# A channel mixer in rounds of two pairs of blocks, its first operands made during the output projection

## The chip, the cores and the metric

The kernel runs on one core of one Trainium2 chip. The core has a matrix engine TensorE (PE, with its weight loads listed as PEld), three engines for elementwise work, VectorE (DVE), ScalarE (ACT) and GpSimd (POOL), and SyncE (SP), whose queue issues the kernel's transfers in program order. The metric is the time of one launch on the device in microseconds (us).

## The reference

One layer of an encoder over 2048 tokens of width 1024, in float32: two kinds of attention side by side, one output projection over both, and a channel mixer with hidden width 4096.

```python
mixed = jnp.concatenate([out_a, out_b], axis=-1)      # attention A and B, 2048 x 1024
x = x + jnp.einsum('bse,ed->bsd', mixed, w_out[l])
h = rmsnorm(x, mlp_norm_g[l])
u = jnp.einsum('bsd,df->bsf', h, w_up[l])
u = jnp.square(jax.nn.relu(u))
x = x + jnp.einsum('bsf,fd->bsd', u, w_down[l])
```

`rmsnorm(x, g)` is x / sqrt(mean(x²) + 1e-6) · g over the width. The result must agree with float32, so each operand of a product is split into a high part `hi` (ACT cast) and the rest `lo` (DVE subtraction), and a product is three matmuls: hi·hi, hi·lo, lo·hi.

## The kernel before

Projections and attention come first and take the time up to about 1820 us. The diff touches what follows.

**Output projection** (`out_proj`). 8 chunks of 256 tokens, two blocks of 128 each. For a chunk, 8 slices `m_raw` are loaded from DRAM, scaled by factors that PE spreads over the partitions (`pr`, lines 662 and 667) and split into `m_hi`, `m_lo`. For a block, 48 matmuls (`py`, line 680) of 128x512 give two halves of the row, DVE adds them to `xo` (line 684), the sum goes to DRAM (`x_d`), is squared and summed by ACT (line 156), multiplied in place by scale and gain (line 161), transposed by PE in eight pieces (`pt`, line 166), copied to `h_f` (lines 691 and 693) and stored to `hb_d`. A scheduler sets the order of instructions on each engine here; a pool with one or two buffers makes a tile wait until its readers are done.

**Channel mixer.** Both products use a Winograd form of Strassen's scheme: a 2x2 block product takes 7 products instead of 8, with operands that are sums of blocks. The 2x2 blocks of the transposed h are B11 to B22, their sums T1 to T4; the sums are formed by POOL from blocks that are loaded again (`h_raw`, `mlp_sums`), stored as `ht_d`, and loaded as operands `hop_T`, `hop_B` of 1 MB, which are split in place.

`mlp_up` (written in its own order, with no scheduler). 32 units: 2 halves of 1024 tokens by 16 slices of w_up. Each unit has 7 products of 12 matmuls (`psX`, `psY`, `psZ`, line 789). w_up of a unit comes as one transfer `wu_raw` of 1 MB, its sums `w_sum` are made by POOL (lines 718 to 721), 7 operands are split into `wu_hi`, `wu_lo` one unit ahead. DVE and ACT evict, square, and POOL sums of the results go to `us_d`. At the first unit four operands are loaded (`hop_T` three times, `hop_B`); in the last unit of the first half all seven are loaded anew.

`mlp_down` (its own order too). 7 right operands of 16 pieces, 8 blocks of tokens for each: 56 steps of 48 matmuls (`pd`, line 1001). In a step `u_raw` of 1 MB for the step after next is loaded, that of the next is split, and pieces of the next right operand are made: one in each of steps 1 to 6 and ten in the last. A piece of a T operand is a difference of two weight blocks, taken by POOL (line 951; T2 has two, lines 947 and 948, and goes to `wt_d`, from where T4 reads it).

## Time and profile before

| | |
|---|---|
| time, median of 3 runs | 3384.73 us (3384.37 to 3384.82) |
| the profiled execution | 3386.51 us, span 3384.70 us |
| PE busy | 3227.7 us, 95% |
| DVE, ACT, POOL busy | 60%, 45%, 48% |
| mean granted PE clock | 0.97 |

A busy share says how much of a time an engine has instructions under way. The granted clock is the share of full speed that PE was given: 1.00 is 2.4 GHz. In the timeline, a bracket behind an instruction names the time for which the engine had stood, and what it waited for. The name left of an arrow in a row is the tile written, those to its right are read; SPq is SyncE's queue.

### The profile page before, as it was taken

How to read it: one execution, taken by the hardware profiler on the slowest of the kernel's cores; microseconds unless marked ns; L12 is line 12 of the kernel's file. 1: busy time of each engine (PE TensorE's matmuls, PEld its weight loads, DVE VectorE, ACT ScalarE, POOL GpSimd, SP SyncE). 2: the span in 40 equal slices, each digit the busy share in tenths (PEclk: the TensorE clock that was granted, in tenths of full speed). 3: DMA queues.
4: the chain of work that ended last, by engine and by line, in shares of the span. 5: the costliest groups of instructions: out<-in, count | busy, mean ns of one | idle time of the engine just before them, and what ended most of it. 6: DMA issues, size and time to landing. Idle time of an engine off the chain costs nothing. (4 is left out here: it accounts for less than half of the span.)

```text
span 3384.7 us, 43164 instructions
## 1 busy us (share of the span) xinstructions
PE 3227.7 (95%) x15584; PEld 2459.7 (73%) x15584; DVE 2042.2 (60%) x3800; ACT 1530.4 (45%) x2344; POOL 1631.6 (48%) x894
## 2 busy tenths in 40 slices
PE   7999989999999999999999985999799999999999
PEld 6888866666666666666667774888688878788887
DVE  6545547777877777777866554554555544546542
ACT  4222226666666666666664222444444443222221
POOL 3344425666676666666665114556466521234200
PEclk9999989999999999999998997999899999899999
DMA  6336290122112210211113677455555465855653
GB/s 202 105 103 210 87 248 15 30 60 81 29 38 76 68 29 29 68 41 29 30 50 122 216 221 230 137 153 156 190 152 156 140 211 186 287 209 203 216 190 103
DMA packets 407894, 431.91 MB, mean 128 GB/s; under 512 B 26080, under 2 KB 343648, under 8 KB 395776
## 3 DMA queue, kind: packets, MB, share of 16 engines
q1 hardware_dynamic: 407680, 429.16, 40.7%
q8 instruction: 122, 2.00, 0.2%
q14 instruction: 92, 0.75, 0.1%
HBM read 287.45 MB, written 150.01 MB: 129 GB/s over the span
## 5 line engine op out<-in xcount | busy, mean ns | idle before, releaser
L545 POOL TENSOR_TENSOR acc<-acc,pta 128x1024 f32<-128x1024 f32 x224 | 535.1, 2389 | 258.6 <-ACT pta L543 253.7
L421 DVE CUSTOM_DVE_ANT_0 Sm<-ps_s,T 128x512 f32<-128x512 f32 x512 | 338.2, 685 | 124.9 <-PE ps_s L416 122.8
L543 ACT ACTIVATE pta<-ps_a 128x512 f32<-128x512 f32 x512 | 292.3, 594 | 208.9 <-PE ps_a L542 195.9
L509 DVE TENSOR_REDUCE mxa<-ps_m 128x1 f32<-128x512 f32 x512 | 330.5, 682 | 59.2 <-PE ps_m L506 57.6
L441 POOL TENSOR_TENSOR Sm<-Sm 128x2048 f32<-128x2048 f32 x64 | 294.4, 4600 | 139.0 <-ACT Sm L440 139.0
L1001 PE MATMUL pd<-wd_lo,u_hi 128*128 128x512 f32 x896 | 353.7, 395 | 6.0 <-DVE wd_lo L150 5.8
L1001 PE MATMUL pd<-wd_hi,u_hi 128*128 128x512 f32 x896 | 352.2, 393 | 7.2 <-ACT wd_hi L149 6.9
L1001 PE MATMUL pd<-wd_hi,u_lo 128*128 128x512 f32 x896 | 351.4, 392 | 2.5 <-DVE u_lo L150 2.5
L416 PE MATMUL ps_s<-Kb,Qb 128*128 128x512 f32 x1024 | 307.1, 410 | 2.4 <-DVE mx L421 2.3
L432 ACT ACTIVATE Sm<-Sm,negm 128x2048 f32<-128x2048 f32 x128 | 256.6, 2005 | 88.1 <-DVE negm L430 80.4
L552 PE MATMUL po_a<-pta,v_a 128*64 128x512 f32 x1024 | 279.7, 620 | 1.9 <-ACT pta L543 1.8
L541 PEld LDWEIGHTS ps_a<-Qa,Ka 128*128 128x128 f32 x512 | 96.2, 188 | 228.4 <-issue 196.3
L149 ACT CAST u_hi<-u_raw 128x1024 fp32r<-128x1024 f32 x112 | 112.2, 1050 | 311.9 <-PE pd L1001 277.8
L541 PE MATMUL ps_a<-Qa,Ka 128*128 128x512 f32 x512 | 233.6, 457 | 17.7 <-DVE vt L150 13.6
L789 PE MATMUL psY<-hop_T,wu_hi 128*128 128x512 f32 x768 | 237.6, 391 | 5.3 <-DVE u L799 5.3
L150 DVE TENSOR_TENSOR tl<-ptb,th 128x512 fp32r<-128x512 f32 x256 | 175.2, 684 | 79.7 <-ACT th L149 79.6
L470 PE MATMUL po_b<-th,Vb 128*128 128x256 f32 x1024 | 209.9, 288 | 9.3 <-ACT th L149 9.0
L416 PEld LDWEIGHTS ps_s<-Kb,Qb 128*128 128x128 f32 x1024 | 179.8, 191 | 47.4 <-DVE mx L421 11.0
L506 PE MATMUL ps_m<-Ka,Qa 128*128 128x512 f32 x512 | 202.5, 435 | 5.8 <-DVE mx L421 1.2
L470 PEld LDWEIGHTS po_b<-th,Vb 128*128 128x128 f32 x1024 | 173.1, 191 | 44.0 <-ACT th L149 14.7
L1001 PEld LDWEIGHTS pd<-wd_lo,u_hi 128*128 128x128 f32 x896 | 169.5, 189 | 48.9 <-DVE wd_lo L150 14.2
L1001 PEld LDWEIGHTS pd<-wd_hi,u_hi 128*128 128x128 f32 x896 | 169.4, 189 | 46.4 <-ACT wd_hi L149 11.3
(231 smaller groups left out, 7445.0 us busy)
## 6 DMA issues: line engine op xcount, KB each, us to landing
u_raw<-us_d SPq DMA_DIRECT2D x56, 1024.0 KB, 5.8
wd_raw<-in_w_down SPq DMA_DIRECT2D x176, 256.0 KB, 5.6
wu_raw<-in_w_up SPq DMA_DIRECT2D x32, 1024.0 KB, 5.9
us_d<-us SPq DMA_DIRECT2D x128, 256.0 KB, 3.4
us_d<-c SPq DMA_DIRECT2D x96, 256.0 KB, 3.8
Qb<-qkT_d SPq DMA_DIRECT2D x128, 128.0 KB, 3.0
Qa<-qkT_d SPq DMA_DIRECT2D x48, 256.0 KB, 4.8
m_raw<-mix_d SPq DMA_DIRECT2D x96, 128.0 KB, 3.6
```

The costliest lines, as they stand in the source:

```text
L416: nc.tensor.matmul(ps, Q[:, c, i, qb * P : (qb + 1) * P], K[c][:, ks], start=(i == 0), stop=(i == 1))
L421: nc.vector.tensor_tensor_reduce(out=Sm[:, ks], in0=ps, in1=T[t0][:, o - t0 : o - t0 + 512], scale=1.0, scalar=BIGNEG, op0=ALU.add, op1=AL ...
L432: nc.scalar.activation(Sm, Sm, AF.Exp, bias=negm, accum_out=l)
L441: nc.gpsimd.tensor_tensor(Pm[0], Pm[0], Pm[1], ALU.add)
L470: nc.tensor.matmul(po, V[a][:, kb, :], b[:, kk, :], start=(kb == 0 and n == 0), stop=(kb == NT - 1 and n == 2),)
L509: nc.vector.tensor_reduce(mx[:, kk : kk + 1], ps, AX.X, ALU.max)
L541: nc.tensor.matmul(ps, K[:, ks], Q[:, i, :], start=True, stop=False)
L543: ex = nc.scalar.activation(pt[:, i, :], ps, AF.Exp)
L545: nc.gpsimd.tensor_tensor(acc, prev if kb == 1 else acc, pt, ALU.add)
L552: nc.tensor.matmul(po[i * HD : (i + 1) * HD, :], v_a[:, kb, g * HD : (g + 1) * HD], pt[:, i, :], start=(kb == 0), stop=(kb == NT - 1),)
L789: nc.tensor.matmul(ps, w[:, j, :], b[:, h, j, :], skip_group_check=not start, start=(start and j == 0 and k == 0), stop=(j == 3 and k == 2),)
L1001: nc.tensor.matmul(ps, a[:, k, :], w, start=(k == 0 and q == 0), stop=(k == NK - 1 and q == 2))
```

## The change

Output projection: a chunk's operands are made one chunk before its blocks (`prepare`), the norm scale goes by ACT from `xt` into `h_f`, the gain is a column multiplied in behind the transposes, `h_f` has one buffer instead of two; sums are formed from `h_f` and two blocks loaded earlier (`h_old`) instead of four loaded again. The first two tiles of w_up and three operands are loaded and split in this stage; three products (36 matmuls) stand before the last block's transposes.

Up projection: pairs of units run in rounds of 14 items, the first three products of both and then the last four of both (`ROUND`). Operands of the left are split 8 items ahead, results are stored 2 to 5 items late. The four late operands of the first half are loaded at the start of `mlp_up` and split at items 2, 4, 5 and 6; those of the second half are loaded one by one behind the product that used them last, and split 5 items later. The last round loads and splits the first operands of the down projection.

Down projection: another order of the right operands; T2's weights are computed in the first 16 steps; additions with U and the second subtraction of T2 are POOL's; loads of pieces are spread over steps, and pairs use two buffers `wd_b`. Pools are taken from both ends of SBUF. The numbers of matmuls stay: 768, 2688 and 2688.

```diff
-            m2b, xp, hp, gp = pool("om_b", 1), pool("ox", 2), pool("oh", 2), pool("og", 1)
-            stage, m2a, mp, sm = pool("ows", 1), pool("om_a", 1), pool("om", 7), pool("osm", 2)
...
+            m2b, xp, hp, hsp, stage = pool("om_b", 1), pool("ox", 2), pool("oh", 1), pool("ohs", 3), pool("ows", 1)
...
+                chunks[tc_] = mh, ml
...
+            def block(tc_, b, before=None):
...
+                if before:
+                    before()
+                self.dma(self.x1_d[rows, :], xt)
+                hf = hp.tile([P, ND, P], F32, name="h2_f")
+                flat = hf.rearrange("p j t -> p (j t)")
+                ss = small.tile([P, 1], F32, name="h2_ss")
+                nc.scalar.activation(flat, xt, AF.Square, accum_out=ss)
+                r = self.rstd(small, ss, 1, 1.0 / D, "h2")
+                nc.scalar.activation(flat, xt, AF.Copy, scale=r)
+                def put(half, pt):
+                    sl = slice(half * 4, half * 4 + 4)
+                    g = gain[:, sl].rearrange("p (j o) -> p j o", o=1).broadcast_to([P, 4, P])
+                    nc.vector.tensor_tensor(hf[:, sl, :], pt, g, ALU.mult)
+                self.transposes(flat, pst, put)
+                c, th, s_ = r0 // 1024, (r0 // 512) % 2, (r0 // P) % 4
+                ts = slice(s_ * P, s_ * P + P)
+                for dh in range(2):
+                    self.dma(self.hb_d[c, 2 * dh + th, :, :, ts], hf[:, dh * 4 : dh * 4 + 4, :])
+                if th:
+                    old = stage.tile([P, 2, 4, P], F32, name="h_old", tag="stage")
                     for dh in range(2):
+                        self.dma(old[:, dh], self.hb_d[c, 2 * dh, :, :, ts])
+                    new = lambda: hsp.tile([P, 4, P], F32, name="h_sum")
+                    done = lambda i, t: self.dma(self.ht_d[c, i, :, :, ts], t)
+                    self.right_sums(old[:, 0], hf[:, 0:4], old[:, 1], hf[:, 4:8], new, done)
...
+            prepare(0)
+            for tc_ in range(8):
+                if tc_ < 7:
+                    prepare(tc_ + 1)
+                else:
+                    self.mlp_begin(early)
                 if tc_ == 4:
+                    self.up_load(0)
+                    self.up_load(1)
+                    self.B[0] = {n: self.operand(0, n) for n in self.RIGHT[:3]}
+                if tc_ == 5:
+                    self.up_sums(0, 0)
+                    self.up_sums(0, 1)
+                    self.up_sums(1, 0)
+                block(tc_, 0)
+                block(tc_, 1, self.mlp_first if tc_ == 7 else None)
...
+    LEFT = ("A11", "A12", "S2", "S3", "S1", "S4", "A22")
+    RIGHT = ("B11", "B21", "T2", "T3", "T1", "B22", "T4")
...
+        if n in self.RIGHT[:3]:
+            t = self.first.tile([P, 2, 4, 512], F32R, name=f"hop_{n}", tag="big")
+        else:
+            t = self.big.tile([P, 2, 4, 512], F32R, name=f"hop_{n}", tag="big")
...
+    ROUND = [(e, i) for lo, hi in ((0, 3), (3, 7)) for e in range(2) for i in range(lo, hi)]
+    def item(self, s):
+        d, r = divmod(s, 14)
+        e, i = self.ROUND[r]
+        return 2 * d + e, i
...
+    def up_split(self, s):
+        if s < 14 * self.NF:
+            n, i = self.item(s)
+            t = self.small_slot().rearrange("p h (j f) -> p h j f", f=P)
+            self.split(t[:, 0], t[:, 1], self.ops[n][self.LEFT[i]])
+            self.W[s] = t
...
+    def mlp_begin(self, early):
+        early.close()
+        self.wop = [self.right("uw", 7)]
+        self.acc = [self.right("psua", 3, space=PSUM)]
+        for s in range(7):
+            self.up_split(s)
+    EARLY = (0, 1, 3)
+    def mlp_first(self):
+        for s in self.EARLY:
+            self.up_product(s)
...
+        for s in self.EARLY:
+            after(s)
+        for n in self.RIGHT[3:]:
+            self.B[0][n] = self.operand(0, n, both=False)
+        splits = {2: "T3", 4: "T1", 5: "B22", 6: "T4"}
+        for s in range(7, 9):
+            self.up_split(s)
+        d = 14
+        done = 14 * (self.NF - 1)
+        for s in range(last + 1):
+            n, i = self.item(s)
+            r, n0 = s % d, 2 * (s // d)
+            if s not in self.EARLY:
+                self.up_product(s)
+                if s == last:
+                    self.down_early(r)
+                after(s)
+            if s > 0:
+                self.up_split(s + 8)
+            if s in splits:
+                self.in_place(self.B[0][splits[s]])
+            if r == 0:
+                self.up_sums(n0 + 1, 1)
+            elif r == 1:
+                self.up_load(n0 + 2)
+            elif r == 5:
+                self.up_load(n0 + 3)
+                self.up_sums(n0 + 2, 0)
+                self.up_sums(n0 + 2, 1)
+            elif r == 8:
+                self.up_sums(n0 + 3, 0)
+            if n == self.NF - 1:
+                name = self.RIGHT[i]
+                t = self.operand(1, name, both=False)
+                self.B.setdefault(1, {})[name] = t
+                later(s + 5, lambda t=t: self.in_place(t))
+            if done <= s < last:
+                self.down_early(r)
+            for f in todo.pop(s, ()):
+                f()
+        for k in range(10, 16):
+            self.fill_piece(0, k)
+        for s in sorted(todo):
+            for f in todo[s]:
+                f()
+    ORDER = ("B11", "B21", "B22", "T2", "T3", "T1", "T4")
...
+    TERMS = {"B11": ("11",), "B21": ("21",), "B22": ("22",), "T2": ("00",), "T3": ("22", "12"), "T1": ("12", "11"), "T4": ("21", "00")}
...
+    def prepare_piece(self, i, k):
+        terms = self.TERMS[self.ORDER[i]]
+        a = self.da.tile([P, 512], F32, name="wd_a")
+        self.dma(a, self.w_down(terms[0], k)[:, 0])
+        if len(terms) > 1:
+            b = self.db.tile([P, 512], F32, name="wd_b")
+            self.dma(b, self.w_down(terms[1], k)[:, 0])
+            self.nc.gpsimd.tensor_tensor(a, a, b, ALU.subtract)
+        self.pending[i, k] = a
+    def prepare_early(self, k):
+        t = self.raws.tile([P, 4, 512], F32, name="wd_raw", tag="raw")
+        self.dma(t, self.w_down(self.TERMS[self.ORDER[0]][0], k, 4))
+        for q in range(4):
+            self.pending[0, k + q] = t[:, q, :]
...
+    def u_load(self, m):
+        if m < len(self.STEPS):
+            i, b = self.STEPS[m]
+            t = self.first.tile([P, 2, 4, 512], F32R, name="u_op", tag="big")
+            self.U[m] = t.rearrange("p h a (k t) -> p h (a k) t", t=P)
+            self.dma(self.U[m][:, 1], self.us_d[self.RIGHT.index(self.ORDER[i]), b])
+    def u_split(self, m):
+        if m < len(self.STEPS):
+            self.in_place(self.U[m])
+    def down_early(self, r):
+        if r in (3, 4, 5):
+            self.u_load(r - 3)
+        if r in (2, 6, 10):
+            self.prepare_early({2: 0, 6: 4, 10: 8}[r])
+        if r in (6, 8):
+            self.u_split(r // 2 - 3)
+        for k in {7: (0, 1), 8: (2,), 9: (3,), 10: (4,), 11: (5,), 12: (6,), 13: (7, 8, 9)}.get(r, ()):
+            self.fill_piece(0, k)
+        if r == 13:
+            self.prepare_early(12)
...
+                if n != "B22":
+                    plus(t, t, U[b], nc.gpsimd)
...
+            def t2(k):
+                a, b, c = self.da.tile([P, H], F32, name="wd_a"), *(self.db.tile([P, H], F32, name="wd_b") for _ in range(2))
+                self.dma(a, self.w_down("12", k)[:, 0])
+                self.dma(b, self.w_down("11", k)[:, 0])
+                self.dma(c, self.w_down("22", k)[:, 0])
+                nc.gpsimd.tensor_tensor(a, a, b, ALU.subtract)
+                nc.gpsimd.tensor_tensor(a, c, a, ALU.subtract)
+                return lambda: self.dma(self.wt_d[k], a)
+            behind = []
+            for m, (i, b) in enumerate(self.STEPS):
+                if m:
+                    self.u_load(m + 2)
+                if m < 16:
+                    behind.append(t2(m))
+                if i < 6:
+                    for k in (6, 7) if b == 6 else (b,) if b < 6 else ():
+                        self.prepare_piece(i + 1, k)
+                    for k in {5: (8, 9, 10), 6: (11, 12), 7: (13, 14, 15)}.get(b, ()):
+                        self.prepare_piece(i + 1, k)
+                if m:
+                    self.u_split(m + 1)
+                if i < 6:
+                    for k in range(6, 16) if b == 7 else (b - 1,) if b else ():
+                        self.fill_piece(i + 1, k)
```

PE at the end of the output projection, before: `py` is the projection's result, `pt` the transposes of the last two blocks, `psX` the first product of the up projection.

```order
L680 MATMUL py<-wo_hi_17869,m_hi 128x512
L680 MATMUL py<-wo_lo_17870,m_hi 128x512
L680 MATMUL py<-wo_hi_17869,m_lo 128x512
L166 MATMUL pt<-ident,xo 128x128 x16
L789 MATMUL psX<-hop_B_19342,wu_hi 128x512 x2
L789 MATMUL psX<-hop_B_19342,wu_lo 128x512
```

PE at the same place, now (`w_op` is a split operand of w_up, `hop_B` and `hop_T` the operands of h):

```order
L691 MATMUL py<-wo_hi_17872,m_lo 128x512
L846 MATMUL psY<-hop_B_19261,w_op 128x512 x12
L846 MATMUL psX<-hop_B_19265,w_op 128x512
L171 MATMUL pt<-ident,h_f 128x128 x8
L846 MATMUL psX<-hop_B_19265,w_op 128x512 x11
L846 MATMUL psY<-hop_B_19261,w_op 128x512 x12
L171 MATMUL pt<-ident,h_f 128x128 x8
L846 MATMUL psY<-hop_T_19269,w_op 128x512 x12
L846 MATMUL psX<-hop_B_19265,w_op 128x512 x12
L846 MATMUL psY<-hop_T_19269,w_op 128x512 x12
L846 MATMUL psY<-hop_T_20218,w_op 128x512 x12
L846 MATMUL psZ<-hop_T_20220,w_op 128x512 x12
```

Three products now stand ahead of the last transposes and between them; the transposes of the last block come after 36 matmuls, and `hop_T_20218`, the first late operand (T3), is the fourth item behind them.

SP in the output projection, before, about two blocks whose sums are formed:

```order
L55 DMA xo<-in_x 128x1024
L55 DMA ht_d<-h_sum 512x1x128
L55 DMA hb_d<-h_f 512x1x128 x2
L55 DMA ht_d<-h_sum 512x1x128
L55 DMA x_d<-xo 128x1024
L55 DMA ht_d<-h_sum 512x1x128
L55 DMA h_raw<-hb_d 128x4x128
L55 DMA ht_d<-h_sum 512x1x128
L55 DMA h_raw<-hb_d 128x4x128
```

SP there, now:

```order
L58 DMA hb_d<-h_f 512x1x128
L58 DMA m_raw<-mix_d 128x256
L58 DMA hb_d<-h_f 512x1x128
L58 DMA ht_d<-h_sum 512x1x128
L58 DMA x_d<-xo 128x1024
L58 DMA m_raw<-mix_d 128x256
L58 DMA ht_d<-h_sum 512x1x128 x2
L58 DMA m_raw<-mix_d 128x256
L58 DMA ht_d<-h_sum 512x1x128
L58 DMA hop_T_19269<-ht_d 128x2048
```

The four `h_raw` loads behind a store are gone; `hb_d` of a block still stands among the stores of sums of the block before it.

SP from the last blocks to the up projection's operands, before:

```order
L55 DMA hb_d<-h_f 512x1x128
L55 DMA h_raw<-hb_d 128x4x128
L55 DMA ht_d<-h_sum 512x1x128 x2
L55 DMA h_raw<-hb_d 128x4x128
L55 DMA ht_d<-h_sum 512x1x128
L55 DMA wu_raw<-in_w_up 128x8x256
L55 DMA ht_d<-h_sum 512x1x128 x4
L55 DMA wu_raw<-in_w_up 128x8x256
L55 DMA hop_T_20174<-ht_d 128x2048
L55 DMA hop_T_20182<-ht_d 128x2048
L55 DMA hop_T_20190<-ht_d 128x2048
L55 DMA hop_B_20198<-hb_d 128x2048
```

SP there, now:

```order
L58 DMA hb_d<-h_f 512x1x128 x2
L58 DMA ht_d<-h_sum 512x1x128 x4
L58 DMA h_old<-hb_d 128x4x128 x2
L58 DMA hb_d<-h_f 512x1x128 x2
L58 DMA ht_d<-h_sum 512x1x128 x4
L58 DMA hop_T_20218<-ht_d 128x2048
L58 DMA hop_T_20220<-ht_d 128x2048
L58 DMA hop_B_20222<-hb_d 128x2048
L58 DMA hop_T_20224<-ht_d 128x2048
L58 DMA wu_raw<-in_w_up 128x8x256
```

The transfers of w_up are no longer between the last sums and the operands; the late operands still come behind the last four stores of sums.

## Rows read from the trace of the kernel before

**Rows 1.** Page, part 1: busy us and share of the span, of each engine
```profile
PE 3227.7 (95%) x15584; PEld 2459.7 (73%) x15584; DVE 2042.2 (60%) x3800; ACT 1530.4 (45%) x2344; POOL 1631.6 (48%) x894
```

**Rows 2.** Stretches: from:to, length, busy us (records) by engine, PE clock, DMA share, GB/s
```profile
2735.00:2780.00 45.00, 38.52 (x147) 27.68 (x146) 26.71 (x29) 22.37 (x34) 6.26 (x4) 0.92 0.80 279
...
2915.00:2970.00 55.00, 48.69 (x180) 35.30 (x179) 32.80 (x36) 15.13 (x20) 18.46 (x13) 0.84 0.86 304
2970.00:3190.00 220.00, 220.00 (x972) 182.19 (x971) 115.58 (x108) 59.57 (x76) 70.24 (x43) 1.00 0.58 203
3190.00:3230.00 40.00, 37.09 (x161) 29.53 (x160) 25.69 (x27) 13.83 (x19) 11.90 (x8) 1.00 0.67 239
...
2400.00:2470.00 70.00, 52.28 (x197) 41.12 (x196) 41.23 (x35) 33.17 (x44) 34.94 (x21) 0.85 0.61 207
2470.00:2735.00 265.00, 265.00 (x1171) 219.43 (x1170) 132.44 (x163) 125.11 (x220) 157.02 (x107) 1.00 0.50 147
2060.00:2130.00 70.00, 31.90 (x124) 25.29 (x125) 31.35 (x31) 24.38 (x34) 32.85 (x22) 0.71 0.62 200
```

**Rows 3.** Chain of waits, up projection: start, us, engine, result, line, instructions
```profile
2455.32 2.72 PE psX L789 x12
```

**Rows 4.** Timeline of PE: start, us, instruction, in brackets the idle time before
```profile
2059.20 0.40 PE L680 MATMUL py<-wo_hi,m_lo 128*128 128x512 f32 x1
2061.08 1.09 PE L166 MATMUL pt<-ident,xo 128*128 128x128 f32 x8 [1.48 <-DVE xo L161]
```

**Rows 5.** Waits of PE, 1980 to 2460: us in total, times, longest
```profile
PE psX L789 <- ACT wu_hi L149: 17.0, 1, 17.0
PE psX L789 <- ACT p L837: 16.6, 2, 10.5
PE pt L166 <- DVE xo L161: 9.4, 2, 8.0
```

**Rows 6.** Timeline of DVE, 1850 to 1863: end of the first block
```profile
1850.53 0.69 DVE L684 TENSOR_TENSOR xo<-py,xo 128x512 f32<-128x512 f32 x1 [0.68 <-PE py L680]
```

**Rows 7.** Groups by line, output projection, 1850 to 2060: busy, mean ns, idle before
```profile
L680 PE MATMUL py<-wo_hi,m_hi 128*128 128x512 f32 x240 | 98.6, 411 | 7.8 <-ACT m_hi L149 6.1 <-DVE xo L684 1.5
...
L161 DVE SCALAR_TENSOR_TENSOR xo<-xo,h_r,g_mlp 128x1024 f32<-128x1024 f32 x15 | 19.9, 1324 | 51.9 <-DMA x_d<-xo 51.9
...
L156 ACT ACTIVATE h_f<-xo 128x1024 f32<-128x1024 f32 x15 | 15.9, 1062 | 38.5 <-DVE xo L684 31.9 <-DMA hb_d<-h_f 3.2 <-DMA xo<-in_x 2.3
```

**Rows 8.** DMA issues, 1850 to 2060: count, KB, median us to landing
```profile
hb_d<-h_f SPq DMA_DIRECT2D x28, 256.0 KB, 4.5
```

**Rows 9.** Timeline of all engines, 2088.4 to 2100: the late operands
```profile
2088.45 2.41 SPq L55 DMA_DIRECT2D hop_T<-ht_d  x3
...
2097.68 1.90 ACT L149 CAST hop_T<-hop_T 128x2048 fp32r<-128x2048 f32 x1 [3.51 <-DMA hop_T<-ht_d]
...
2099.61 2.29 DVE L150 TENSOR_TENSOR hop_T<-hop_T 128x2048 fp32r<-128x2048 f32 x1 [2.14 <-ACT hop_T L149]
```

**Rows 10.** DMA issues, 2395 to 2450: operands of the second half
```profile
hop_T<-ht_d SPq DMA_DIRECT2D x4, 1024.0 KB, 13.8
```

**Rows 11.** Page, part 6: DMA issues of the weights, down projection
```profile
wd_raw<-in_w_down SPq DMA_DIRECT2D x176, 256.0 KB, 5.6
```

**Rows 12.** Groups by line, down projection, 2750 to 3380
```profile
L951 POOL TENSOR_TENSOR wd_raw<-wd_raw 128x512 f32<-128x512 f32 x48 | 78.5, 1643 | 146.5 <-DMA wd_raw<-in_w_down 77.2 <-DMA wd_raw<-wt_d 66.6 <-DVE wd_lo L150 2.5
...
L891 DVE TENSOR_TENSOR x<-x,U 128x512 f32<-128x512 f32 x24 | 19.2, 798 | 0.8
```

**Rows 13.** Groups by line, up projection, 2470 to 2735: w_sum on POOL
```profile
L720 POOL TENSOR_TENSOR w_sum<-wu_raw 128x512 f32<-128x512 f32 x13 | 16.9, 1298 | 25.0 <-DVE wu_lo L150 25.0
```

**Rows 14.** Timeline of POOL, 2097 to 2112
```profile
2102.59 3.25 POOL L720 TENSOR_TENSOR w_sum<-wu_raw 128x512 f32<-128x512 f32 x1 [3.70 <-DVE wu_lo L150]
```

**Rows 15.** Timeline of all engines, 1957 to 1966: end of put, stores
```profile
1957.61 0.68 DVE L691 COPY h_f<-pt 128x512 f32<-128x512 f32 x1
...
1965.13 1.33 SPq L55 DMA_DIRECT2D hb_d<-h_f  x2
```

More of the change, by code (lines that the diff above doesn't have):

```diff
@@ L150, in split, with norm_transpose @@
         self.nc.vector.tensor_tensor(lo, src, as32(hi), ALU.subtract)
-    def norm_transpose(self, xt, out, pool, pst, name, put, gain=None):
+    def norm_transpose(self, xt, out, pool, pst, name, put):
         nc = self.nc
@@ L582, in row_sums, with out_proj @@
         nc.vector.reciprocal(l, l)
[L585 removed]
+    def out_proj(self):
         nc, tc, ap = self.nc, self.tc, self.ap
@@ new lines, in fill_piece @@
+    def fill_piece(self, i, k):
+        if not self.quad(i, k):
+            self.D[i, k] = self.small_slot()
+        elif k % 4 == 0:
+            t = self.big.tile([P, 2, 4, 512], F32R, name="wd_q", tag="big")
+            for q in range(4):
+                self.D[i, k + q] = t[:, :, q, :]
+        w = self.D[i, k]
+        self.split(w[:, 0], w[:, 1], self.pending.pop((i, k)))
+    STEPS = [(i, b) for i in range(7) for b in range(8)]
+    def u_load(self, m):
[4 more added lines that the diff above has]
+            self.dma(self.U[m][:, 1], self.us_d[self.RIGHT.index(self.ORDER[i]), b])
@@ L898, in x1 @@
                     return None
-                half, dh = goes[order[i]]
+                half, dh = goes[n]
                 t = xp.tile([P, H], F32, name="x1")
                 self.dma(t, self.x1_d[rows(half, b), dh * H : dh * H + H])
+                if n != "B22":
+                    plus(t, t, U[b], nc.gpsimd)
                 return t
             def finish(i, b, ps, t):
-                n = order[i]
+                n = self.ORDER[i]
+                store = lambda half, dh, t: (lambda: self.dma(out[0, rows(half, b), dh * H : dh * H + H], t))
@@ L917, in finish @@
[L917 to L919 removed]
+                    if n == "T2":
+                        plus(y12[b], y12[b], U[b], nc.gpsimd)
                 else:
                     plus(t, ps, t)
[L922 removed]
                     if n == "T1":
                         plus(y12[b], ps, y12[b])
[L925 to L928 removed]
@@ L1004, in build @@
+                for f in behind:
+                    f()
+                behind = finish(i, b, ps, x)
+            for f in behind:
+                f()
     def build(self):
```

445 lines of the change are left out of this document (187 added, 258 removed).

## The prediction

> **What bounds the kernel now.** I read the engine table first: TensorE (PE) is busy for 95% of the span, so time can only come from the places where it is idle or slowed [rows 1]. I looked for these with the view by stretches, over everything behind the attention [rows 2]. In a clean stretch PE's busy time equals the stretch and the granted clock is 1.00; such are 2470 to 2735 and 2970 to 3190. There the chain of waits has one unit, 12 matmuls in 2.72 us [rows 3], or 0.2267 us for a matmul. The loss of another stretch is its length less its matmuls at that pace:
> - 2060 to 2130, the passage from the output projection to the up projection: 124 records, of which 12 are transposes (16 of them, 2.2 us by the row of eight [rows 4]): 70 − 112 × 0.2267 − 2.2 = 42.4 us.
> - 2400 to 2470, between the two token halves of the up projection: 70 − 197 × 0.2267 = 25.3 us.
> - 2735 to 2780, up to down: 45 − 147 × 0.2267 = 11.7 us.
> - 2915 to 2970 and 3190 to 3230, two changes of the right operand in the down projection: 14.2 and 3.5 us.
>
> The sum is 97 us, all of it in four kinds of places, with nothing lost between. The PE waits name who came last: in the first two stretches wu_hi once for 17.0 us, p twice for 16.6, the transposes on xo 9.4 [rows 5]. p and wu_hi are no true causes: they sit on ACT and DVE behind operands that were loaded late.
>
> The output projection is the fifth place. The sums of its first block reach DVE at 1850.5 [rows 6], its last matmul ends at 2059.6 [rows 4]: 15 blocks in 209 us, 13.9 each. The matmuls of one are 48 × 0.2267 = 10.9; eight transposes cost about 1.1 and the share of the scale transposes about 1.1, so the floor is 13.1, and 12 us are lost. Half of it is one wait for m_hi of 6.1 [rows 7].
>
> **The change, part by part.** The matmuls are the same in number (768, 2688, 2688), so only waits can go or come.
>
> *Output projection.* A chunk's operands are prepared one chunk ahead: the wait of 6.1 for m_hi goes. The norm scale is no longer multiplied in place on xo, which waited 51.9 us in all for the store of x1 [rows 7]; ACT writes it into h_f. Against it h_f has one buffer instead of two, so a block's chain is now a loop: square 1.1 and read-out 0.2, mean and power about 1, scaling about 1.1, transposes 1.1, two multiplications of 0.7, then the stores of hb_d at 4.5 [rows 7, 8]. That is 10.4 us with handovers left out, some 11 to 12 with them, below the 13.1 of PE. In the half of the blocks that form sums, h_f is also held by three GpSimd subtractions of 1.3, beside the store. I give it 8 us of stalls over the 15 blocks, and 15 × 13.1 + 8 = 204.5 for 209. At the head, the first block now follows the attention whole, without about 40 of its matmuls between the attention's last ones; but its weights are split earlier and its scales need no low-clock interleaving. By the order I let it end 9 us earlier, bounds 5 later and 15 earlier. Sum: 14 earlier (0 to 28).
>
> *Output to up projection.* Before, PE stood for the xo chain, then for the loading of w_up, which was issued after the last block, then for four late operands. Now three products (36 matmuls, 8.2 us) stand right behind the last py, with weights and operands that are loaded during the output projection; the last transposes come behind them, at 8.2 + 1.1 = 9.3 us. The last block's square has to wait for h_f of the block before: its transposes stand behind 13 matmuls (end at 4), two multiplications 1.4 and the store 4.5 to 5 make 10.5; square, power and scale 3.5 more: PE waits about 4.7 and leaves the transposes at 15. Three further products end at 23.3; then T3 is needed. T3 is loaded behind the last four stores of ht_d: transposes 15, multiplications 1.4, four subtractions 1.3 to 1.7 with their stores and landing, so issued at about 24. Before, from the issue of the operands at 2088.45 to the cast were 9.2 us, and 4.2 more until lo was ready [rows 9]; T3, first of four, should take 6 and 4.2: ready at 34. A stall of 10.5. With a lower clock after the two stalls (before, 0.71 in this stretch [rows 2]) another 2.5 to 5. That leaves about 20 of the 42.4 and of the 1.5 before the first transposes [rows 4]: 24 us gained (10 to 38).
>
> *Between the halves.* Before, seven operands were reloaded in a burst and needed at once. Now each is loaded behind the product that used its buffer last, is split 5 items (13.6 us) later, and used 10 or 11 items after the load. The loads took up to 13.8 us when four ran together [rows 10]: about in time for the split, with 13.6 us behind it as reserve. I leave 2 of 25.3: 23 gained (10 to 25).
>
> *Up to down.* The first 16 weight pieces and three u operands are loaded and split within the last round, ten before its end. Of 11.7 I leave 2: 10 gained (0 to 12).
>
> *Down projection.* Ten of an operand's 16 pieces are still split in the last step before its border. But they are loaded over the last three steps, not three pieces ahead, and what is T2's weight is computed early and kept in DRAM. The second members of pairs go through two buffers of wd_b: a pair needs its load, 5.6 us [rows 11], and a GpSimd subtraction of 1.64 [rows 12]; two at a time that is 3.6 us a pair, so 8 to 10 pairs at steps 5 to 7 take 29 to 36 of 32.6 us. SyncE's queue stands meanwhile, and the next u operand stands behind it. With 0 to 5 us at each of six borders I reckon 2, 4, 0, 4, 4, 5, or about 19, less 4 for what the free buffers let run ahead: 15 after 17.7: gain 3 (from a loss of 37, as rival 1 has it, to 17). Also, the additions x1 + U, 24 of 0.8 us on DVE [rows 12], and the second subtraction for T2 go to GpSimd.
>
> Here a rule speaks against the change. GpSimd and VectorE get in each other's way in this trace: a GpSimd subtraction of w_sum takes 1.30 on average in a clean stretch and 3.25 beside DVE's lo subtraction of an operand, which takes 2.29 [rows 9, 13, 14]. The Trainium skill (SBUF — State Buffer, Who interferes with whom) says that the shared port pair is an exclusive lock: the one who comes second is blocked for the whole of the other's instruction. The trace agrees: 3.25 − 1.30 is 1.95, most of such an instruction of the other engine. By that rule the moved additions give VectorE nothing back at a border; the rival on the borders below prices it from rows.
>
> Sum: 14 + 24 + 23 + 10 + 3 = 74. The profiled execution took 3386.5 us (span 3384.7), so 3312.5; the median of the runs, 3384.7, lies 1.8 below it: 3310.7, I say 3310.
>
> **The rivals.**
> 1. *The borders of the down projection become bound by VectorE and GpSimd.* Ten splits stand in the last step; if each lo is held by half a GpSimd operation of 1.64 [rows 12], a border is 8 us later, six borders 48; with what is left of the loads' waits, about 55 stand for the 15 assumed. For it: ten fills at one step. Against: before had ten at the border too, and stood only 17.7 us. Time 3310 + 40 = 3350.
> 2. *The single h_f makes the output projection slower, and the kernel slower than before.* In SyncE's in-order queue hb_d of one block was issued at 1965.1, though the last copy into h_f ended at 1958.3, since it stood behind other stores and loads [rows 15]. If that 7 us enters every loop, it is 11.5 + 7 = 18.5 instead of 13.1: 5.4 for each of 16 blocks, 86 us. It decides from 1.6 us of queueing per block on. Against: the h_raw loads, which fed ht_d, go, and the next h_old load stands in the queue ahead of its need. Time 3310 + 86 = 3396.
> 3. *Everything is hidden.* All places fall to the transposes' wait alone: 97 + 20 = 117 gained, time 3386.5 − 117 − 1.8 = 3268. For it: each operand has over 10 us of reserve. Against: T3 depends on the last block's sums, whatever its buffer.
> 4. *The change does not do what it says* at the halves, since splits in place back up on ACT and DVE (seven of 1.9 and 2.3 us in 14 items) and delay the evictions: 15 of the 23 us come back, 3325.
>
> **How the numbers follow.** My forecast has 0.52, rival 3 0.13, rival 4 0.15, rival 1 0.11, rival 2 0.09. What can be told from no change is 0.2%, 6.8 us. The range goes from 3272 to 3348: it holds the forecast's own bounds, rival 4 and half of rivals 1 and 3. Rival 2 gives slower, 0.07, and same, 0.02; rival 1 can with other small misses reach same, 0.02. Faster is 0.89, same 0.04, slower 0.07.
>
> **What would show it.** In the changed trace: the first psY behind the last py without a gap; one gap of 4 to 6 us at the last transposes, and one of about 10 at the first product with T3 (psY); PE full at the change of halves; gaps of 0 to 5 us at the borders of the down projection, on wd_hi, wd_lo or the u operand's halves; a block of the output projection every 13 to 14 us. If blocks come every 18 us with square waiting for hb_d, rival 2 holds; if lo at a border takes 1.7 and more and PE waits 10 us there, rival 1. The forecast is wrong if the stretch behind the last py loses over 35 us, or the down projection over 40.

## The result, and the profile after

The changed kernel takes 3361.62 us (median of 4 runs, 3357.71 to 3364.84) against 3384.55 for the kernel before on the same chips: a ratio of 0.9932, interval 0.9915 to 0.9949. It is faster by 23 us; the forecast was a gain of 74. The profiled execution of after, which the accounts below use, took 3357.71 us, 28.8 less than the one of before.

The engine table of after, the answer to [rows 1]:

```profile
PE 3238.4 (96%) x15584; PEld 2459.6 (73%) x15584; DVE 2043.7 (61%) x3672; ACT 1576.0 (47%) x2352; POOL 1716.8 (51%) x934
```

The same 15584 instructions keep PE busy 10.7 us longer than before, in a shorter span and with a higher mean granted clock (0.981 for 0.973). That is the first sign that a matmul itself has become longer. The stretches of after, as [rows 2] (from:to, length, busy us and records by engine, PE clock, DMA share, GB/s): the output projection, the passage to the up projection, the change of halves, up to down, one piece of the down projection with stalls and one without.

```profile
1850.00:2044.00 194.00, 194.00 (x979) 161.50 (x978) 107.12 (x225) 66.57 (x119) 50.97 (x49) 1.00 0.71 223
2040.00:2130.00 90.00, 76.03 (x305) 59.76 (x304) 45.41 (x45) 41.07 (x64) 43.07 (x31) 0.91 0.60 190
2380.00:2440.00 60.00, 51.57 (x214) 41.05 (x213) 42.77 (x38) 37.24 (x58) 33.62 (x22) 0.94 0.45 133
2690.00:2720.00 30.00, 26.17 (x95) 18.42 (x94) 21.32 (x19) 15.44 (x26) 13.58 (x8) 0.89 0.68 202
2900.00:2960.00 60.00, 54.52 (x225) 43.20 (x224) 20.82 (x20) 16.40 (x15) 3.83 (x3) 0.94 0.57 206
3020.00:3140.00 120.00, 120.00 (x518) 97.37 (x518) 53.40 (x41) 32.30 (x30) 43.89 (x25) 1.00 0.49 172
```

The last line is the important one. PE is busy for all of 120 us, at a granted clock of 1.00, yet it has 518 records; at the pace of [rows 3] there would be 529. A stretch without a gap is not a stretch without a loss. The timeline of PE shows it by the distance of the starts (start, us, instruction, count). After, in the up projection:

```profile
2464.59 2.95 PE L846 MATMUL psY<-hop_B,w_op 128*128 128x512 f32 x12
2467.38 2.96 PE L846 MATMUL psX<-hop_B,w_op 128*128 128x512 f32 x12
2470.18 2.96 PE L846 MATMUL psY<-hop_T,w_op 128*128 128x512 f32 x12
2472.98 2.96 PE L846 MATMUL psY<-hop_B,w_op 128*128 128x512 f32 x12
...
2484.12 2.88 PE L846 MATMUL psZ<-hop_T,w_op 128*128 128x512 f32 x12
2486.84 2.88 PE L846 MATMUL psV<-hop_B,w_op 128*128 128x512 f32 x12
2489.56 5.60 PE L846 MATMUL psY<-hop_T,w_op 128*128 128x512 f32 x24
```

The first three products of the two units of a pair start 2.80 us apart (233.3 ns for a matmul), the later ones 2.72 (226.7 ns). The slow ones are those whose operands of h lie in the pool of the three early operands (`first` in the diff); the fast ones use the four late operands (`big`). Before, all of the up projection was at 226.7. In the down projection of after every matmul is slow (232.4 on average).

Loss is counted from here on by the starts of PE: the distance to the next start less 0.2267 us for a matmul of 512 columns (a proportional share for narrower ones). Where one distance exceeds that by more than 20 ns it is a stall, so that a matmul at the lower level of the clock counts as one; else the excess is put under pace.

| us lost | before | forecast leaves | after |
|---|---|---|---|
| output to up projection | 45.0 | 20 | 22.5 |
| change of halves | 25.6 | 2 | 11.1 |
| up to down | 11.9 | 2 | 8.6 |
| stalls in the down projection | 18.6 | 15 | 22.7 |
| pace of the matmuls | 0.5 | 0 | 22.8 |
| end of the last py (at 2059.6 before, 2044.2 after) | | 14 earlier | 15.4 earlier |

The gains are 15.4 + 22.5 + 14.5 + 3.3 − 4.1 − 22.3 = 29.3, against 28.8 between the two executions. Against the forecast about 49 us more are lost in the first five rows; pace is almost half of that.

What ended PE's waits after, as [rows 5], in three windows (us in total, times, longest; the longest rows of each): output to up (2040 to 2130), halves (2370 to 2440), and the down projection from 2715 to 2960.

```profile
PE psY L846 <- ACT uy L915: 4.5, 1, 4.5
PE psY L846 <- DVE hop_T L154: 3.3, 2, 1.8
PE pt L171 <- ACT h_f L705: 2.7, 1, 2.7
```
```profile
PE psY L846 <- ACT uy L915: 7.6, 2, 6.3
```
```profile
PE pd L1147 <- ACT wd_q L153: 5.0, 1, 5.0
PE pd L1147 <- DVE u_op L154: 3.5, 3, 2.3
PE pd L1147 <- ACT w_op L153: 3.1, 1, 3.1
```

The wait for the transposes shrank from 9.4 [rows 5] to 2.7. uy is the copy by which ACT empties a PSUM bank: PE waits for a free bank at the halves, not for an operand.

### The profile page after: what moved, and what is told of

It reads as the page before. It is cut to its first block, busy times and chain, and to the rows that moved or that the text cites. A ratio compares the mean times of both kernels' runs of the same rounds, so it can differ in the third digit from the quotient of the medians.

```text
span 3355.9 us, 43068 instructions
## 1 busy us (share of the span) xinstructions
PE 3238.4 (96%) x15584; PEld 2459.6 (73%) x15584; DVE 2043.7 (61%) x3672; ACT 1576.0 (47%) x2352; POOL 1716.8 (51%) x934
## 5 line engine op out<-in xcount | busy, mean ns | idle before, releaser
L1147 PE MATMUL pd<-wd_q,u_op 128*128 128x512 f32 x1728 | 416.1, 399 | 10.0 <-ACT wd_q L153 5.6
L1147 PEld LDWEIGHTS pd<-wd_q,u_op 128*128 128x128 f32 x1728 | 328.4, 191 | 91.9 <-ACT wd_q L153 6.5
L846 PE MATMUL psY<-hop_T,w_op 128*128 128x512 f32 x1152 | 281.0, 398 | 17.2 <-ACT uy L915 12.1
L846 PEld LDWEIGHTS psY<-hop_T,w_op 128*128 128x128 f32 x1152 | 219.6, 191 | 68.8 <-ACT uy L915 14.2
L546 PEld LDWEIGHTS ps_a<-Qa,Ka 128*128 128x128 f32 x512 | 96.3, 189 | 228.8 <-issue 196.6
L153 ACT CAST u_op<-u_op 128x2048 fp32r<-128x2048 f32 x56 | 106.7, 1907 | 309.4 <-DMA u_op<-us_d 309.4
L546 PE MATMUL ps_a<-Qa,Ka 128*128 128x512 f32 x512 | 233.2, 456 | 17.3 <-DVE vt L154 12.6
L1147 PE MATMUL pd<-w_op,u_op 128*128 128x512 f32 x960 | 234.9, 399 | 7.9 <-ACT w_op L153 4.8
L154 DVE TENSOR_TENSOR w_op<-w_sum,w_op 128x512 fp32r<-128x512 f32 x128 | 151.8, 1197 | 137.8 <-ACT w_op L153 137.7
L1147 PEld LDWEIGHTS pd<-w_op,u_op 128*128 128x128 f32 x960 | 182.2, 190 | 53.5 <-ACT w_op L153 6.0
```

The source lines that it names most:

```text
L154: self.nc.vector.tensor_tensor(lo, src, as32(hi), ALU.subtract)
L546: nc.tensor.matmul(ps, K[:, ks], Q[:, i, :], start=True, stop=False)
L846: self.nc.tensor.matmul(ps, w[:, wk, j, :], b[:, h, j, :], skip_group_check=not start, start=(start and j == 0 and k == 0), stop=(j == 3 a ...
L1147: nc.tensor.matmul(ps, u[:, h, k, :], w[:, g, :], start=(k == 0 and q == 0), stop=(k == NK - 1 and q == 2))
```

## The experiments

**Why a matmul takes 233 ns.** From the memory map of the two compiled programs I took where each operand starts within a partition. Before, stationary and moving operands of the up and down projections start at addresses that are equal modulo 256 bytes. After, the early operands (the first buffer at 18016, where the operands of u lie later) differ by 128 modulo 256 from the weights at the other end (200672, 192480); the late operands (126944) do not. These addresses stand in no trace. Theory A: this difference sets the pace. Theory B: it is not the address, but the traffic or the order around the matmuls. The first kernel leaves out the layer and holds only matmuls on copies of one input tile, 36 for each pair of addresses, with one transfer loaded ahead of them all (...: lines left out; CASES lists the pairs of start addresses):

```
for i, (w0, m0) in enumerate(CASES):
    ...
    w, m = w0 // 4, m0 // 4
    ...
    for r in range(REPS):
        for j in range(4):
            for wk, mk in ((0, 0), (0, 1), (1, 0)):
                ws = w + wk * 512 + j * 128
                ms = m + mk * 2048 + j * 512
                nc.tensor.matmul(pt, big[:, ws : ws + 128], big[:, ms : ms + 512], ...)
```

> Leaves out the whole layer and runs only 32 groups of 36 matmuls of 128x512, each group with another placement of the stationary and the moving operand in one large tile, and one group again at the end. Theory A (the pace of a matmul depends on where its two operands lie to each other, by the difference of their addresses modulo 256 bytes): groups with a difference of 0 take 226 to 228 ns a matmul, those with 128 take 232 to 234, others lie between; multiples of 256 change nothing. Rival B (the pace of the changed kernel is slowed by what other engines and transfers do at the time): all 32 groups take the same 226 to 228 ns, since nothing else runs.

Mean spacing of the starts in a group (one execution, without the first three of each group), by the moving operand's address minus the stationary operand's, modulo 256:

| difference | 0 | 32 | 64 | 96 | 128 | 160 | 192 | 224 |
|---|---|---|---|---|---|---|---|---|
| ns, moving operand shifted | 226.7 | 233.4 | 229.0 | 233.7 | 233.3 | 234.4 | 233.3 | 233.3 |
| ns, stationary operand shifted | 227.0 | 233.3 | 228.8 | 233.2 | 232.4 | 234.4 | 233.3 | 233.3 |

A further 256, 512, 1024 or 2048 bytes change nothing, nor does a shift of both operands together: the ten groups at difference 0 lie at 226.7 to 227.5. (The group run first is left out; its first matmuls start up to 0.59 us apart.) Beside these matmuls there is only the copy and store of the result of the group before, the same for every pair of addresses, so theory B has fallen as the cause of a slow pace. Next the same in the two kernels, by 128 unused bytes, the pad: in after behind the constants, in before between the two operands.

```
 after:   self.lns = pool.tile([P, 1], F32, name="lns")
+         pad = pool.tile([P, 32], F32, name="pad")
+         nc.vector.memset(pad, 0.0)
 before:  pool = self.pools(es)          # up projection; likewise ahead of the
+         pad = pool("upad", 1).tile([P, 32], F32, name="pad")   # weights of down
          wop, vp, later = pool("uw", 9), ...
...
```

> The changed kernel with one unused tile of 128 bytes per partition behind the constants, which shifts all pools of the left end against those of the right end. Theory A: the 1152 matmuls of the up projection that read the first three operands go from 233.3 to 226.7 ns and the 2688 of the down projection from 232.4 to 226.7: 7.6 + 15.3 = 23 us less than the changed kernel, about 3338. Rival B: no change, 3357 to 3365.

> The kernel before with an unused 128 bytes between the operands of h and those of w_up, and between those of u and of w_down. Theory A: three of seven products of the up projection and all of the down projection go to 232 to 233.5 ns: 1152 x 6.6 ns + 2688 x 5.7 to 6.6 ns = 23 to 25 us slower, about 3408. Rival B: 3384.6 as before.

Measured: after with the pad 3351.93 us (ratio to before 0.9895, 0.9880 to 0.9909), before with the shift 3408.01 (1.0067, 1.0052 to 1.0082). Before becomes 22 us slower, as A has it. The chain of waits in a stretch of the down projection without stalls (start, us, instructions) for before, before shifted, after, and after with the pad:

```profile
2999.84 40.35 PE pd L1001 x178
```
```profile
2999.83 40.21 PE pd L1005 x173
```
```profile
2959.80 50.43 PE pd L1147 x217
```
```profile
2959.78 50.32 PE pd L1149 x222
```

That is 226.7, 232.4, 232.4 and 226.7 ns for a matmul. With the pad, pace falls from 22.8 to 0.4, but the time by 10 only instead of 23: the stalls rise from 65 to 78, those of the down projection from 22.7 to 34. A faster PE runs into what feeds it there. All later kernels except one stand on the pad.

**What feeds the down projection.** SyncE issues all loads in order. Its two longest waits from 2696 to 2960, after:

```profile
SPq L58 <- POOL wd_a L1121: 107.6, 14, 9.1
SPq L58 <- PE pd L1147: 30.3, 4, 9.9
```

In 14 places it stands for the second GpSimd subtraction of a T2 weight, whose store (wt_d) is at the head of the queue, with the next u operand behind it. The timeline of after shows one such place and what it costs (start, us, engine; in brackets the idle time before):

```profile
2870.62 1.62 POOL L1121 TENSOR_TENSOR wd_a<-wd_b,wd_a 128x512 f32<-128x512 f32 x1
2872.27 0.33 SPq L58 DMA_DIRECT2D wt_d<-wd_a  x1
2872.65 0.43 SPq L58 DMA_DIRECT2D x<-x_d  x1
2873.19 0.37 SPq L58 DMA_DIRECT2D u_op<-us_d  x1
```
```profile
2878.64 1.91 ACT L153 CAST u_op<-u_op 128x2048 fp32r<-128x2048 f32 x1 [9.66 <-DMA u_op<-us_d]
2880.58 2.97 DVE L154 TENSOR_TENSOR u_op<-u_op 128x2048 fp32r<-128x2048 f32 x1 [2.86 <-ACT u_op L153]
2883.60 6.71 PE L1147 MATMUL pd<-wd_q,u_op 128*128 128x512 f32 x21 [2.28 <-DVE u_op L154]
```

Released at 2872.2, u_op is issued at 2873.2, cast at 2878.6, split by 2883.55, and PE goes on at 2883.60. Two edits, each on the pad: the T2 weights earlier, two to a step (steps 0 to 4 and 8 to 11); or left in place, with the store one step later, behind that step's load of u.

```
+            EARLY_T2 = {0: (0, 1), 1: (2, 3), 2: (4, 5), 3: (6, 7), 4: (8,), 8: (9, 10), 9: (11, 12), 10: (13, 14), 11: (15,)}
...
-                if m < 16:
-                    behind.append(t2(m))
+                for k in EARLY_T2.get(m, ()):
+                    behind.append(t2(k))
```

> The pad of e2, and T2's weights computed in steps 0 to 4 of the first two right operands (two a step) instead of one in each of the first 16 steps. Theory E (the first two borders of the down projection, 9.1 us each in e2, and the 4.7 between them come from the loads of the last three pieces, which wait for buffers that T2's weights hold in steps 5 to 7): the two borders fall to 0 to 3 us each, 12 to 18 us less than e2 in all, about 3337. Rival F (the borders come from VectorE and GpSimd blocking each other): the borders stay at 7 to 9 us, since the work of both engines is the same.

```
-            behind = []
+            behind, stores = [], []
...
                 if m:
                     self.u_load(m + 2)
+                for f in stores:
+                    f()
+                stores = []
                 if m < 16:
-                    behind.append(t2(m))
+                    stores.append(t2(m))
```

> The pad of e2; the store of a T2 weight (wt_d) is issued one step later, behind the next step's load of u, one weight in each of the first 16 steps as in the changed kernel. Theory H (in the first 16 steps SyncE's in-order queue stands at the store of wt_d, which waits for two GpSimd subtractions, and the next u operand is loaded behind it): the losses inside these steps (0.9, 4.7 and 1.8 us in e2, on u_op) go, those at the two borders (9.1 each, on the last pieces) stay or fall a little: 5 to 10 us less than e2, about 3344. Rival E (the buffers of the last steps alone): the losses on u_op stay.

Earlier: 3352.52 (0.9899, 0.9882 to 0.9915), no change against the pad alone, where 12 to 18 us less were expected; the first two borders (a border is the change from one right operand to the next) lose nothing any more, but the steps with T2 weights lose 7.2 + 2.8 + 6.7 + 8.0, all on u_op. Later store: 3328.01 (0.9823, 0.9806 to 0.9840), 24 us less than the pad alone, where 5 to 10 were expected. The borders, which I had put down to their ten fills (splits of weight pieces), are among what went: those near 2800 and 2900 fall from 9.1 each to 1.0 and 1.4. Their stretch with the pad alone, and with the later store:

```profile
2880.00:2940.00 60.00, 52.57 (x218) 41.83 (x217) 24.32 (x23) 19.20 (x20) 9.61 (x6) 0.94 0.64 228
```
```profile
2880.00:2940.00 60.00, 58.88 (x260) 48.41 (x259) 22.89 (x20) 15.80 (x14) 3.50 (x3) 1.00 0.56 203
```

SyncE's wait for GpSimd falls with it:

```profile
SPq L58 <- PE pd L1152: 91.7, 17, 10.8
SPq L58 <- POOL wd_a L1123: 34.9, 10, 6.8
```

SyncE still waits, but for PE, which frees buffers: the queue is now ahead of its consumer. Both parts apart, to see what each is worth without the other: the later store on after without the pad.

> The changed kernel without any pad, only with the store of each T2 weight issued behind the next step's load of u (as in e7). Theory H: the stalls of the first 24 steps of the down projection, about 21 us in the changed kernel, go, and the pace of 232 ns stays: about 3341. If the pad and the store only help together (a faster TensorE was needed before feeding counts, or the other way about), it stays above 3352.

Measured 3342.45 (0.9869, 0.9853 to 0.9886): 19 us less than after, stalls of the down projection 22.7 to 1.7, pace not cured at 24.8. So the pad alone gives 10, the store alone 19, both 34. Two refinements on both: T2 weights only in the steps 0 to 4 of the first three operands, where no fills stand; and on top of that 192 bytes ahead of the even chunks' operands of the output projection, the stationary ones there: wo, the moving operand, lies 64 modulo 256 below them, a difference of 192 in the order of the table (for the odd chunks it is 0).

```
-                if m < 16:
-                    stores.append(t2(m))
+                if i < 3 and b < 5:
+                    stores.append(t2(5 * i + b))
+                elif m == 13:
+                    stores.append(t2(15))
```

> e7, and one T2 weight in each of steps 0 to 4 of the first three right operands and one at step 5 of the second, none in the last two steps before a border. Theories H and E together: losses on u_op gone, the two borders at 0 to 3 us each: the first 24 steps lose under 5 us where e2 loses 25, about 3332. If only H holds, the borders keep 9 us each and the time is that of e7.

```
-            mp, sm, m2a = pool("om", 6), pool("osm", 2), pool("om_a", 1)
+            mp, sm, padp, m2a = pool("om", 6), pool("osm", 2), pool("omp", 1), pool("om_a", 1)
+            pad = padp.tile([P, 48], F32, name="pad")
```

> e8 with 192 unused bytes ahead of the even chunks' operands m_hi and m_lo in the output projection, so that they differ from w_out's by a multiple of 256 bytes like the odd ones'. Theory A: the 8 blocks of even chunks go from 233 to 228 ns a matmul: 384 x 5.5 ns = 2 us less than e8. Rival: no change that can be told.

Measured 3322.76 (0.9809, 0.9791 to 0.9826) and 3322.65 (0.9807, 0.9791 to 0.9822). The first takes another 5 in the median, of which the trace shows 3 in the down projection: only the last border is left, with 7.1 for 10.3 in all. The second brings the blocks of even chunks from 233.3 to some 229 ns, and the 15 blocks behind the first from 195.5 us to 193.9; the 2 us expected cannot be seen in the total. These two are the best versions: 63 us below before on the same chip and 39 below after.

**The change of halves.** With the pad the loss there is 8.4 + 1.2 + 1.7 = 11.3, nearly all one wait for uy. VectorE's timeline just ahead of it, after (with the pad the same records take the same times, within 0.01 us):

```profile
2366.06 1.38 DVE L154 TENSOR_TENSOR w_op<-w_sum,w_op 128x512 fp32r<-128x512 f32 x1 [1.87 <-ACT w_op L153]
2367.87 2.86 DVE L154 TENSOR_TENSOR hop_B<-hop_B 128x2048 fp32r<-128x2048 f32 x1 [0.44 <-ACT hop_B L153]
2370.66 1.79 DVE L154 TENSOR_TENSOR w_op<-wu_raw,w_op 128x512 fp32r<-128x512 f32 x1
2372.37 3.38 DVE L154 TENSOR_TENSOR hop_B<-hop_B 128x2048 fp32r<-128x2048 f32 x1
2375.67 1.78 DVE L154 TENSOR_TENSOR w_op<-wu_raw,w_op 128x512 fp32r<-128x512 f32 x1
2377.37 3.38 DVE L154 TENSOR_TENSOR hop_T<-hop_T 128x2048 fp32r<-128x2048 f32 x1
2380.68 0.68 DVE L888 TENSOR_TENSOR c<-psZ,uy 128x512 f32<-128x512 f32 x1
```

From 2367.9 VectorE is busy for 13 us without a pause; the addition that reads PSUM comes at 2380.7, behind the three operand splits and three weight splits of the rows above it, each 0.6 to 1.1 us longer than elsewhere (0.69 and 2.29). ACT's copy uy stands in order behind work that waits for that addition. Two theories: the three splits in a row are the burden (C), or GpSimd's work beside them, which makes them longer (G). First, the splits of two operands apart:

```
-                later(s + 5, lambda t=t: self.in_place(t))
+                later(s + (5, 6, 7, 5, 6, 6, 7)[i], lambda t=t: self.in_place(t))
```

> The pad of e2 and, between the token halves, the splits of the reloaded operands two items apart instead of one (5, 6, 7 and 5, 6, 6, 7 items behind their loads). Theory C (the 11.5 us lost there come from VectorE, where three splits stand in a row and evictions wait behind them): the loss falls to 2 to 4 us, 7 to 9 us less than e2. Rival D (the operands land too late): the loss stays or grows, the wait of TensorE then being for the operands hop_T or hop_B.

Then the GpSimd work taken away around the halves and the end of the up projection, in two doses: the block sums of six units, then also the weight sums of five. Unsummed blocks stand in for them, so the output differs there; what is read is the time alone.

```
         def sub(a, b, op=ALU.subtract):
+            if self.quiet:
+                return a
...
+            self.quiet = n in (14, 15, 16, 17, 30, 31)
```

> The pad of e2 without the GpSimd sums of the results (S1 to S4) for units 14 to 17 and 30 to 31; their unsummed parts are stored instead, so the output differs there. Theory G (the losses between the halves, 11.3 us in e2, and from up to down, 9.1, come from VectorE's subtractions, which GpSimd's sums lengthen from 0.69 to 1.7 and from 2.29 to 3.4): the lo of hop_B and hop_T take 2.3 to 2.9, those of w_op 0.7, and the two losses fall to 0 to 4 us each. Rival D (the order of splits and evictions on ACT and VectorE alone): the losses stay above 7 us each.

```
+        if n in (15, 16, 17, 18, 19):
+            self.ops[n] = {"A11": a11, "A12": a12, "A22": a22, "S1": a21, "S2": a22, "S3": a11, "S4": a12}
+            return
```

> e6, and the GpSimd sums of w_up's blocks left out for units 15 to 19 as well (the blocks themselves serve as operands, so the output differs there): GpSimd has nothing to do between the halves. Theory G (GpSimd's share in VectorE's time makes the loss there): of the 11.3 us in e2 and 7.7 in e6, 0 to 3 are left, and the lo of hop_B and hop_T take 2.3. Rival D (the order on ACT and VectorE alone): 6 to 8 are left, though no subtraction is lengthened.

Measured: splits apart 3351.12 (0.9901, 0.9885 to 0.9918), the same as the pad alone, the loss at the halves 7.6 + 4.7 = 12.3; it moved, in part to an operand that is now split later (PE waits 5.0 for uy and 3.0 for hop_B). Without the block sums 3339.28, without both 3333.79 (one execution each); the loss at the halves is 11.3, 7.7 and 4.1. VectorE's timeline in the last one:

```profile
2364.70 0.68 DVE L156 TENSOR_TENSOR w_op<-wu_raw,w_op 128x512 fp32r<-128x512 f32 x1
2365.96 2.29 DVE L156 TENSOR_TENSOR hop_B<-hop_B 128x2048 fp32r<-128x2048 f32 x1 [0.58 <-ACT hop_B L155]
2368.17 0.68 DVE L156 TENSOR_TENSOR w_op<-wu_raw,w_op 128x512 fp32r<-128x512 f32 x1
2368.78 2.29 DVE L156 TENSOR_TENSOR hop_T<-hop_T 128x2048 fp32r<-128x2048 f32 x1
2370.99 0.68 DVE L893 TENSOR_TENSOR c<-psZ,uy 128x512 f32<-128x512 f32 x1
```

The lengthening is gone from every record here. PE's gap at the same place, after, without the block sums, and without both:

```profile
2388.55 4.80 PE L846 MATMUL psY<-hop_T,w_op 128*128 128x512 f32 x12 [6.34 <-ACT uy L915]
```
```profile
2383.69 5.49 PE L848 MATMUL psY<-hop_T,w_op 128*128 128x512 f32 x12 [4.82 <-ACT uy L920]
```
```profile
2378.88 4.45 PE L851 MATMUL psY<-hop_T,w_op 128*128 128x512 f32 x12 [2.26 <-ACT uy L923]
```

So 7.2 of 11.3 us go with GpSimd's work beside VectorE; 4.1 stay, which the order on VectorE and ACT may explain. That was tried on the best version, by splitting the reloaded operands in quarters over four items, so that no long split stands ahead of an eviction:

```
-                later(s + 5, lambda t=t: self.in_place(t))
+                for q in range(4):
+                    later(s + 5 + q, lambda t=t, q=q: self.split(t[:, 0, q], t[:, 1, q], as32(t[:, 1, q])))
```

> e9 with each reloaded operand split in four quarters, at items 5, 6, 7 and 8 behind its load, instead of whole at item 5. Theory I (between the halves the evictions wait behind single long subtractions of 2.3 to 3.4 us in VectorE's queue): the loss of 11.3 us falls to 3 to 6, 5 to 8 us less than e9. Rival J (VectorE and GpSimd have too much work in these items, however it is cut): the loss stays at 9 to 13.

Measured 3328.44 (0.9834, 0.9819 to 0.9848), 6 us slower than without it, and 17.1 lost at the halves for 11.3. PE's waits from 2360 to 2440, without the quarters and with them (the longest of those for an operand, and that for the bank):

```profile
PE psY L850 <- ACT uy L919: 8.1, 3, 6.5
```
```profile
PE psY L850 <- DVE hop_T L156: 2.9, 3, 2.3
PE psY L850 <- ACT uy L919: 1.0, 1, 1.0
```

The wait for the bank is gone but for 1.0, as the order has it; in its place PE waits 8.5 in all for halves of hop_T and hop_B, whose last quarter is split three items later than the whole was, in more instructions beside the same GpSimd work. The edit moved the loss to the operands and so decides nothing on the order. What the 4.1 us are stays open.

## Why the prediction was wrong

- **The step that failed** is the first sentence of the change part: "The matmuls are the same in number (768, 2688, 2688), so only waits can go or come." Pace had no term. The change moved the pools to both ends of SBUF, and with that the operands' start addresses against each other: 22.8 us against 0.5 before, shown both ways (pad −22.4 of pace, shift of before +22 us). No rival held it. The change names the move of memory itself; I gave it no price.
- **The down projection's term, 15 against 22.7**, and its cause. I reckoned that "SyncE's queue stands meanwhile, and the next u operand stands behind it", but at the borders alone, because of their ten fills. By borders the term was further off than by its sum: the first two with the steps between them, given 2 and 4, lost 21.0; the last three, given 4, 4 and 5, lost 1.7. The queue stood in 14 places for T2 weights whose stores are issued ahead of the next load, a place that I had priced only with "T2's weight is computed early and kept in DRAM". Putting the store behind the load leaves 1.7 (after) and 10.3 (with the pad: 1.0 + 1.4 + 7.9). Rival 1, borders bound by VectorE and GpSimd, has fallen: the fills stayed and the first two borders went to 1.0 and 1.4. Only the last border's 7 us might be its share.
- **Halves, 2 against 11.1.** The loads came in time, as I said; the splits backed up in front of the evictions. That is rival 4's mechanism at 9 of its 15 us, and 7.2 of it is not the splits but GpSimd beside them. The row that tells it was in the prediction, 3.25 against 1.30 [rows 13, 14], but I used it for the down projection only, and in one direction: VectorE's 0.69 becomes 1.8 just as well. The rule of the Trainium skill quoted there (SBUF — State Buffer, Who interferes with whom) fits: 3.38 − 2.29 and 1.79 − 0.68 are the same 1.1 us, most of a GpSimd instruction of 1.3, whatever VectorE's own length.
- **Up to down, 2 against 8.6.** GpSimd has a part (9.1 with the pad, 6.1 and 6.4 in the two quiet kernels). Some 6 us stay unexplained; no run took them apart. The trace of after has waits of 3.7 us for split weight pieces there, and a granted clock of 0.72 from 2702 to 2714.
- **Right in its sum, by luck in its parts: the output projection** (14 forecast, 15.4 measured). PE is busy for 194.00 of 194 us, so the single h_f costs PE nothing and rival 2 has fallen. But the 8 us of stalls never came: the 15 blocks behind the first one take 195.2 us for 208.2, 13.0 less where I had 4.5. The head, for which I had 9, gave 2.3 (the first block's last matmul ends at 1849.0 for 1851.4), and that is within the spread: the ten later versions of after, the same up to there but for the pads, have it between 1846.3 and 1853.8.
- **Right in its sum only: the passage to the up projection** (20 left, 22.5 measured). T3 was split 31.3 us behind the last py, where I had 34, but PE waits 2.7 there and not 10.5, since just before it stood 4.5 for a bank, which had no term. The transposes cost 2.7 for 4.7, the other late operands 4.0, and matmuls at the lower level of the clock (0.66 to 0.75 granted in stretches from 2062 to 2090) some 7 for 2.5 to 5. Rival 3, everything hidden, has fallen.

The 49 us missing are therefore 22.8 of pace, 7.7 in the down projection, 9.1 at the halves, 6.6 from up to down and 2.5 behind the output projection. The version of 3322.76 shows that 39 come back by the pad, the later store and the earlier T2 weights.

## What to carry to other kernels

A change that moves pools changes the operands' addresses: compare the stationary and the moving operand's start modulo 256 bytes, and read PE's pace from the distance of starts, since its busy share (120.00 of 120 us) and clock (1.00) showed nothing here. In an in-order queue, put a store that waits for an engine behind the loads that others will need. Price work moved to GpSimd by what it does to VectorE in the same microseconds, and look at what VectorE has to do there for PE.

## What the runs showed of the hardware

- A matmul of 128x512 on 128x128 starts every 226.7 to 227.5 ns when the two operands' start addresses in the partition are equal modulo 256 bytes, every 229 ns when the moving operand's address less the stationary one's is 64, and every 232 to 234 ns at the other multiples of 32, 192 among them: the sign counts. It does not matter which of the two is shifted. The chain of waits for a group of either kind (start, us, instructions), difference 128 and difference 0:

```profile
63.90 7.23 PE case L57 x31
```
```profile
171.79 7.25 PE case L57 x32
```

  Why is open: no run separates the reading of weights from that of the moving operand. The output projection of the real kernels fits the table: in after, blocks of even chunks run at 233.2 to 233.4 at a difference of 192 and those of odd chunks at 227 to 229 at 0; in before, where by the memory map the difference is 64, most blocks run at 229. That the blocks at 0 do not all reach 226.7 is open; transposes stand between their matmuls.
- GpSimd and VectorE on plain two-input subtractions in SBUF: VectorE 0.69 becomes 1.8 and 2.29 becomes 3.38, GpSimd 1.3 becomes up to 3.4, and every lengthening of VectorE at the halves went when GpSimd's work was left out there.
